# High-half products first, low-half products last within each weight piece of a two-layer decoder trunk

## The chip, the core and the metric

The kernel runs on one core of one Trainium2 chip. The metric is the device time of one execution in microseconds (us); the median of three runs is given, with the lowest and the highest beside it. Engines are called by the names of the profile: PE (TensorE, the matrix multiplier), PEld (its loads of the stationary operand), DVE (VectorE), ACT (ScalarE), POOL (GpSimd) and SP (SyncE, which issues most transfers here).

## What is computed

The reference is a decoder trunk with two layers over 256 tokens and a width of 2048, all in float32: a Mamba-2 state-space layer, one shared K/V projection, and a layer of dilated window attention. Almost all of the arithmetic is in seven projections; the rest works on their outputs.

```python
for layer in range(2):
    shift, scale, gate = adaln(c, ada_w[layer], ada_b[layer])       # silu(c) @ w + b, w: 2048 x 6144
    h = x * (1 + scale) + shift
    if layer == 0:                                                   # state-space layer
        z, xBC, dt = split(h @ in_w)                                 # 2048 x 10304
        xs, B, C = split(silu(causal_conv(xBC)))                     # depthwise, 4 taps
        y = ssd_scan(xs * dt, dt * A, B, C) + xs * D_skip            # 8 groups, one chunk of 256
        y = group_rms_norm(y * silu(z)) * norm_g @ out_w             # 4096 x 2048
    else:                                                            # attention layer
        q, z = split(h @ b_in_w)                                     # 2048 x 4096
        o = merge(dilated_attention(q[g], k[g], v[g]) for g in 3)    # by log-sum-exp weights
        y = (o * silu(z)) @ b_out_w                                  # 1024 x 2048
    x = layer_norm(alpha * x + (1 + gate) * y) * ln_g + ln_b
    if layer == 0:
        k, v = split(x @ kv_w)                                       # 2048 x 6144
```

## The kernel before

**Products in halves.** A float32 product is made of three products of the rounded format fp32r. Each operand is split into a high half (the value rounded) and a low half (what the rounding left): high x high, high x low and low x high are added up in one PSUM accumulator. The activations are split once, when they are made (tiles `hhi`/`hlo`, `xhi`/`xlo`, `yhi`/`ylo`, `oghi`/`oglo`, in the profile mostly `actT`). The weights are split as they arrive. `load_piece` (L90) issues a transfer of 512 KB from SP's queue into `raw` (six buffers), and `split` has ACT copy it into the high half `whi` (L100) and then DVE subtract that from `raw` into the low half `wlo` (L102). There are four buffers of each half. A buffer of `raw` is free again after the subtraction; a buffer of a half is free after the last matmul that reads it.

**Three forms of product.** A piece is the unit in which weights arrive and in which matmuls are issued.

- `cm_piece` (L151 to L153) gives columns by tokens: the weights are the stationary operand, the activations (256 tokens) move. A piece holds two k-tiles (`k`, rows of 128) of 512 output columns, in four blocks `n` of 128: 2 x 4 x 3 = 24 matmuls of 256 columns. The accumulator is two PSUM banks with two blocks each. Each block gets its three products one after the other.
- `cm_wide` (L182, L185) gives the same layout, for weights in pieces of four k-tiles and 256 columns. The high and low halves of the activations lie side by side, so one matmul of 512 columns (L182) makes two products, in the two halves of the block's bank; a matmul of 256 columns (L185) adds weight-low x activation-high. Per k-tile there are two of L182 and then two of L185, 16 matmuls a piece. At the end ACT and DVE add the halves of the bank (`put`).
- `tm_mults` (L213 to L215) gives tokens by columns: a block of 128 tokens of the activations is the stationary operand, and the weights (512 columns) move. A piece holds two k-tiles for two token blocks `b`, each with a bank of its own: 2 x 2 x 3 = 12 matmuls of 512 columns.

A product over all k-tiles is a loop over pieces with one accumulator pair (`cm_quad`, `cm_wide`, `tm_chunk`). The next product uses another pair; the pool `mm` has four banks. Near its end a product may begin the split of the next one's first piece (`begin_next`), and evictions are placed behind that split (`behind_next`) or put off into the next product (`later`, `owed`, `settle`).

**The opening stretch.** The first layer's activations `h` are not there at the start. Two columns of 1 MB of adaLN weights per k-tile are fetched, dotted with silu(c) on DVE (L295), and give shift and scale; ACT then writes `htmp` (L500) and the high half `hhi[kt]` (L502), and DVE the low half `hlo[kt]` (L504). Sixteen k-tiles come out one by one. Meanwhile a list written out by hand (`order`) says which pieces of which products use the k-tiles that are there. Each of its rows brings two more k-tiles into use. The names in it are the products: `z0`, `b4`, `x1` and so on, a dot marks the end of a part, whose sum is put away in SBUF (L633, L635), and the two `h` are the pieces of the first B/C and xs products. The last k-tiles are 14 and 15.

**The first layer's scan.** After the opening, `dt` goes through a softplus and a cumulative sum on DVE and small matmuls (L690 to L711); the cumulative rows are written to DRAM (`cumd`) and read back spread over the partitions (`cbc`). From these ACT makes the decay weights `seg` (L734, L736) of each group. `stage1` also transposes xs on PE (L745), and `stage2` makes the group's output (L767, L776). Both are placed between the products of the next groups.

**Order of issue.** The engines each run their instructions in a fixed order. It follows the program's order as far as a planner at build time, with costs of its own, finds the operands and buffers free; where the order matters it is pinned by `tc.issue_after`. So a transpose of a later step can stand between the matmuls of one piece.

Of the kernel before, what the change touches and what calls it, by code (L numbers as in the profile page):

```python
# [18 lines left out]
P = 128  # L19
# [30 lines left out]
def trunk(ctx, tc, xT, x, c, par, cst, bias, lnrow, ada, wdt, win, wxs, wout, wk, wv, wbin, wbout, out):  # L50
    nc = tc.nc
    V, S, T, PO = nc.vector, nc.scalar, nc.tensor, nc.gpsimd
# [35 lines left out]
    def load_piece(src):  # L88
        raw = wp.tile([P, 1024], F32, name="raw", bufs=6)
        nc.sync.dma_start(raw, src)  # L90
        return raw
# [5 lines left out]
    def split(raw, into=None, after=None, off=(0, 0)):  # L97

        hi, lo = into or halves_at(off)
        copied.append(S.activation(hi, raw, AF.Copy))  # L100
        with tc.issue_after(after) if after is not None else ExitStack():
            latest.append(V.tensor_tensor(lo, raw, hi.bitcast(F32), op=ALU.subtract))  # L102
        return hi.rearrange("p (k n) -> p k n", k=2), lo.rearrange("p (k n) -> p k n", k=2)
# [4 lines left out]
    def settle():  # L108

        while owed:  # L110
            with tc.issue_after(copied[-1].ins), tc.issue_after(latest[-1].ins):
                owed.pop(0)()

    def first_or(src, q, off=(0, 0)):

        return ready.pop() if ready else split(load_piece(src[q]), off=off)

    def begin_next():

        if upcoming:  # L120
            src, q, off = upcoming.pop(0)
            ready.append(split(load_piece(src[q]), off=off))

    def behind_next():

        stack = ExitStack()
        if ready:
            stack.enter_context(tc.issue_after(copied[-1].ins))
            stack.enter_context(tc.issue_after(latest[-1].ins))
        return stack  # L130

    def background(n, every=1):

        state[0] += n
        while state[0] >= every and jobs:
            state[0] -= every
            jobs.pop(0)()
# [3 lines left out]
    def cm_piece(src, q, ps, ahi, alo, k0=0, k1=KT, w=None, after=None, ks=(0, 1)):  # L141


        hi, lo = w or split(load_piece(src[q]), after=after, off=SHORT)
        for k in ks:
            kt = 2 * q + k
            for n in range(4):
                o = ps[n // 2][:, n % 2, :]
                c_ = slice(n * P, n * P + P)
                first = kt == k0 and n % 2 == 0  # L150
                T.matmul(o, hi[:, k, c_], ahi[:, kt, :], start=first, stop=False, skip_group_check=True)  # L151
                T.matmul(o, hi[:, k, c_], alo[:, kt, :], start=False, stop=False, skip_group_check=True)  # L152
                T.matmul(o, lo[:, k, c_], ahi[:, kt, :], start=False, stop=kt == k1 - 1, skip_group_check=True)  # L153

    def acc_pair(pool=None):
        return [(pool or mm).tile([P, 2, L], F32, name="acc") for _ in range(2)]
# [11 lines left out]
    def cm_wide(src, dst, rate=(0, 1), moving=None, later=False):  # L168

        both, high = moving or (lambda kt: xp[:, kt], lambda kt: xhi[:, kt, :])  # L170
        ps = acc_pair()
        for q in range(KT // 4):
            w = first_or(src, q, SHORT)
            if q == 1:
                settle()
            if q == KT // 4 - 1:
                begin_next()
            hi, lo = (t.rearrange("p k n -> p (k n)").rearrange("p (k n) -> p k n", k=4) for t in w)
            for k in range(4):
                kt = 4 * q + k  # L180
                for n in range(2):
                    T.matmul(ps[n], hi[:, k, n * P:n * P + P], both(kt), start=kt == 0, stop=False,  # L182
                             skip_group_check=True)
                for n in range(2):
                    T.matmul(ps[n][:, 0, :], lo[:, k, n * P:n * P + P], high(kt), start=False, stop=kt == KT - 1,  # L185
                             skip_group_check=True)
            background(*rate)
        def put():
            for n in range(2):
                S.activation(dst[:, n, :], ps[n][:, 1, :], AF.Copy)  # L190
                V.tensor_tensor(dst[:, n, :], ps[n][:, 0, :], dst[:, n, :], op=ALU.add)

        if later:
            owed.append(put)
        else:
            with behind_next():
                put()
# [7 lines left out]

    def tm_mults(q, w, ps, ahi, alo, k0, k1, blocks, cols=slice(0, 512)):
        hi, lo = (t[:, :, cols] for t in w)
        for k in range(2):
            kt = 2 * q + k
            for b in blocks:  # L210
                h_, l_ = ahi(kt)[:, b * P:b * P + P], alo(kt)[:, b * P:b * P + P]
                o, part = ps[b][:, cols], cols != slice(0, 512)
                T.matmul(o, h_, hi[:, k, :], start=kt == k0, stop=False, skip_group_check=part)  # L213
                T.matmul(o, h_, lo[:, k, :], start=False, stop=False, skip_group_check=part)  # L214
                end = T.matmul(o, l_, hi[:, k, :], start=False, stop=kt == k1 - 1, skip_group_check=part)  # L215
        return end

    def tm_pair():
# [115 lines left out]
    with ExitStack() as cA:  # L334
# [15 lines left out]
        with ExitStack() as cS:  # L350
# [78 lines left out]
            with ExitStack() as c0:  # L429
# [27 lines left out]
                first = [acc_pair(ex), acc_pair(ex)]  # L457
                cols = [(0, kind, kt) for kt in range(KT) for kind in ("scale", "shift")]
# [51 lines left out]
                part = {n: p[1:] for n, p in zip(names, begun.values())}  # L510
                two = "h"
                order = []
                for row in ("b4:0. b6:0. h z2:0. z1:0. b2:0 x1:0 h", "b2:1. x1:1. z1:1. z4:0 h h",
# [3 lines left out]
                    for w in row.split():  # L517
                        if w == two:
                            n = -2 if sum(o[0] == -2 for o in order) == sum(o[0] == -1 for o in order) else -1
# [117 lines left out]
                for i, (k, q, ends) in enumerate(order):  # L637
# [21 lines left out]
                    k0, k1 = (begin[k], 2 * q + 2 if ends else KT) if k in part else (0, KT)  # L659
# [178 lines left out]
            def y_to(ct):  # L838
                if ct < 4:
                    return [t[:, ct, :] for t in y_first]  # L840
                return yhi[ct // 16][:, ct % 16, :], ylo[ct // 4][:, ct % 4, :]
# [65 lines left out]
        for n in range(4):  # L907
            ps = tm_chunk(wout[n], lambda kt: y_to(kt)[0], lambda kt: y_to(kt)[1],
                          nk=2 * KT, rate=(1, 4) if n else (1, 2),
                          pre={0: y_ahead, 3: first_weights}.get(n), split_end=4 if n == 3 else 0)  # L910
# [67 lines left out]
    with ExitStack() as cL:  # L978
# [3 lines left out]
        def high(i, b):  # L982
            for k in range(2):
                kt = 2 * (i // 2) + k
                for w in first_v[i]:
                    T.matmul(vps[i % 2][b], hx(kt)[:, b * P:b * P + P], w[:, k, :], start=kt == 0 and w is first_v[i][0],  # L986
                             stop=False)
# [6 lines left out]
        end, _ = x_quad(0)  # L994
# [192 lines left out]
    for n in range(2):  # L1187
        ps = tm_chunk(wbout[n], *og, nk=H)
# [14 lines left out]
    ps = [tm_pair() for _ in range(2)]  # L1203
# [49 lines left out]
    end = last(1, 1, slice(256, 512), halves[1])  # L1253
# [124 lines left out]
```

## Time and profile before

| | before |
|---|---|
| median of three runs | 1235.47 us |
| lowest and highest | 1234.38 to 1236.19 us |
| profiled execution, span from first to last instruction | 1233.4 us |
| PE busy | 1219.2 us (99%), 7132 matmuls |
| PEld busy | 1048.7 us (85%), 7132 loads |
| DVE busy | 1027.8 us (83%) |
| ACT busy | 701.2 us (57%) |
| mean granted TensorE clock | 1.000 |
| HBM read | 331.45 MB, 271 GB/s over the span |

The page gives no time for the profiled execution but its span; the median of the runs is 2.1 us longer than that span. Matmuls are pipelined and their ends are modelled, so a busy share of 99% says that PE always had a matmul in hand, not that it ran at its peak; how fast it went is read from the steps between the starts of matmuls. In rows of the timeline the first number is the start, the second the time until the end of the group, and `x2` means that two neighbours are put together. In brackets stands the idle time ahead and what ended it.

### The profile page before, as it was taken

The page shows a single profiled execution, that of the slowest core. Times are in us where ns is not written, and L with a number is a line of the kernel's source. Part 1 is how long each engine was busy: PE and PEld are TensorE (multiplying, and loading weights), DVE is VectorE, ACT ScalarE, POOL GpSimd, SP SyncE. Part 2 cuts the span into 40 slices and gives each one's busy share as a digit, 9 for nine tenths or more (in the row PEclk, how much of TensorE's full clock was granted, in tenths as well). Part 3 has the DMA queues.
Part 4 walks back from the last instruction along what each step waited for, and adds up shares of the span by engine and source line. Part 5 has one row for each costly group of instructions (what it writes and reads, how often), then busy time and mean ns, then how long its engine had stood idle before and what let it go on. Part 6 is the DMA issues. An engine that isn't in the chain of part 4 may idle for free.

```text
span 1233.4 us, 18854 instructions
## 1 busy us (share of the span) xinstructions
PE 1219.2 (99%) x7132; PEld 1048.7 (85%) x7132; DVE 1027.8 (83%) x1464; ACT 701.2 (57%) x1048; POOL 3.9 (0%) x8
## 2 busy tenths in 40 slices
PE   8999999999999999999999999999999999999998
PEld 7889988898888888888888788888888888888886
DVE  6999986999988989899768678888978866758776
ACT  4554477878597789764335544434445644445551
POOL 0000000000000000000000000000000000000001
PEclk9999999999999999999999999999999999999999
DMA  9999977687656556698998569989998774464673
GB/s 377 423 420 422 421 255 248 224 299 252 215 199 209 168 171 205 217 338 345 362 316 293 196 202 372 347 344 371 382 384 306 232 256 144 122 199 128 206 257 69
DMA packets 81371, 335.92 MB, mean 272 GB/s; under 512 B 9200, under 2 KB 9984, under 8 KB 68480
## 3 DMA queue, kind: packets, MB, share of 16 engines
q1 hardware_dynamic: 80352, 333.33, 75.0%
q0 software_dynamic: 576, 1.05, 0.6%
q8 instruction: 56, 0.92, 0.3%
q10 hardware_dynamic: 352, 0.34, 0.1%
q14 instruction: 35, 0.29, 0.1%
HBM read 331.45 MB, written 3.23 MB: 271 GB/s over the span
## 4 chain that ended last, share of the span: by engine, by line
PE 81%; DMA 10%; DVE 6%; ACT 2%; issue 1%; DVEq 0%; ACTq 0%; SPq 0%
PE acc L182 24%; PE acc L185 12%; PE acc L214 11%; PE acc L215 11%; PE acc L213 11%; DMA raw<-in_win 5%; DMA araw<-in_ada 3%; DVE wlo L102 2%; DVE araw L295 2%; PE py L776 1%; ACT whi L100 1%; PE acc L151 1%; PE acc L153 1%; PE acc L152 1%; PE acc L986 1%
## 5 line engine op out<-in xcount | busy, mean ns | idle before, releaser
L100 ACT ACTIVATE whi<-raw 128x1024 fp32r<-128x1024 f32 x389 | 408.5, 1058 | 358.7 <-PE acc L215 128.9
L102 DVE TENSOR_TENSOR wlo<-raw,whi 128x1024 fp32r<-128x1024 f32 x389 | 469.2, 1220 | 147.8 <-ACT whi L100 139.1
L182 PE MATMUL acc<-actT,whi 128*128 128x512 f32 x1280 | 402.7, 394 | 0.0
L185 PEld LDWEIGHTS acc<-actT,wlo 128*128 128x128 f32 x1280 | 239.6, 188 | 53.5 <-DVE wlo L102 0.5
L214 PE MATMUL acc<-wlo,actT 128*128 128x512 f32 x656 | 257.4, 392 | 2.8 <-DVE wlo L102 2.8
L185 PE MATMUL acc<-actT,wlo 128*128 128x256 f32 x1280 | 253.8, 280 | 0.0
L213 PE MATMUL acc<-whi,actT 128*128 128x512 f32 x656 | 253.5, 394 | 0.0
L295 DVE SCALAR_TENSOR_TENSOR araw<-araw,cb__72 128x2048 f32<-128x2048 f32 x95 | 217.0, 2284 | 2.9 <-DMA araw<-in_ada 2.6
L182 PEld LDWEIGHTS acc<-actT,whi 128*128 128x128 f32 x1280 | 193.9, 188 | 0.4
L215 PE MATMUL acc<-whi,actT 128*128 128x512 f32 x432 | 168.8, 391 | 0.0
L214 PEld LDWEIGHTS acc<-wlo,actT 128*128 128x128 f32 x656 | 123.2, 188 | 30.3 <-DVE wlo L102 5.1
L213 PEld LDWEIGHTS acc<-whi,actT 128*128 128x128 f32 x656 | 122.6, 188 | 24.2
L151 PE MATMUL acc<-actT,whi 128*128 128x256 f32 x372 | 103.1, 281 | 1.5 <-ACT actT L502 0.9
L153 PE MATMUL acc<-actT,wlo 128*128 128x256 f32 x372 | 101.9, 282 | 1.3 <-DVE wlo L102 1.1
L152 PE MATMUL acc<-actT,whi 128*128 128x256 f32 x372 | 103.1, 280 | 0.0
L215 PEld LDWEIGHTS acc<-whi,actT 128*128 128x128 f32 x432 | 81.1, 188 | 16.5
L215 PE MATMUL acc<-whi,ylo 128*128 128x512 f32 x224 | 87.6, 391 | 0.0
L151 PEld LDWEIGHTS acc<-actT,whi 128*128 128x128 f32 x372 | 69.6, 188 | 2.8 <-ACT actT L502 1.3
L153 PEld LDWEIGHTS acc<-actT,wlo 128*128 128x128 f32 x372 | 68.9, 188 | 2.5 <-DVE wlo L102 2.3
L152 PEld LDWEIGHTS acc<-actT,whi 128*128 128x128 f32 x372 | 70.6, 190 | 0.2
L215 PEld LDWEIGHTS acc<-whi,ylo 128*128 128x128 f32 x224 | 42.1, 188 | 8.5
L734 ACT ACTIVATE seg<-cbc,cumT 128x128 f32<-128x128 f32 x128 | 41.1, 389 | 3.5 <-PE py L776 2.1
(311 smaller groups left out, 1151.8 us busy)
## 6 DMA issues: line engine op xcount, KB each, us to landing
araw<-in_ada SPq DMA_DIRECT2D x96, 1024.0 KB, 7.2
raw<-in_win SPq DMA_DIRECT2D x109, 512.0 KB, 6.5
raw<-in_wout SPq DMA_DIRECT2D x64, 512.0 KB, 5.6
raw<-in_wbin SPq DMA_DIRECT2D x64, 512.0 KB, 3.8
raw<-in_wxs SPq DMA_DIRECT2D x48, 512.0 KB, 4.4
raw<-in_wv SPq DMA_DIRECT2D x48, 512.0 KB, 7.2
raw<-in_wk SPq DMA_DIRECT2D x48, 512.0 KB, 7.8
cbc<-cumd SPq DMA_DIRECT2D x16, 512.0 KB, 5.4
```

The source lines that it names most:

```text
L100: copied.append(S.activation(hi, raw, AF.Copy))
L102: latest.append(V.tensor_tensor(lo, raw, hi.bitcast(F32), op=ALU.subtract))
L151: T.matmul(o, hi[:, k, c_], ahi[:, kt, :], start=first, stop=False, skip_group_check=True)
L152: T.matmul(o, hi[:, k, c_], alo[:, kt, :], start=False, stop=False, skip_group_check=True)
L153: T.matmul(o, lo[:, k, c_], ahi[:, kt, :], start=False, stop=kt == k1 - 1, skip_group_check=True)
L182: T.matmul(ps[n], hi[:, k, n * P:n * P + P], both(kt), start=kt == 0, stop=False, skip_group_check=True)
L185: T.matmul(ps[n][:, 0, :], lo[:, k, n * P:n * P + P], high(kt), start=False, stop=kt == KT - 1, skip_group_check=True)
L213: T.matmul(o, h_, hi[:, k, :], start=kt == k0, stop=False, skip_group_check=part)
L214: T.matmul(o, h_, lo[:, k, :], start=False, stop=False, skip_group_check=part)
L215: end = T.matmul(o, l_, hi[:, k, :], start=False, stop=kt == k1 - 1, skip_group_check=part)
L295: return V.scalar_tensor_tensor(raw, raw, 1.0, cb_, op0=ALU.mult, op1=ALU.mult, accum_out=mod[layer][:, ct, j:j + 1])
L734: S.activation(seg[:, hh, b, :], cbc[:, hh, b, :], AF.Relu, bias=cumT[:, b, h0 + hh:h0 + hh + 1], scale=-1.0)
```

## The change

Within a piece the loops are turned inside out. The outermost loop now goes over the kinds of product, and those with the weights' low half are last:

- `cm_piece`: all weight-high x activation-high of the piece (8 matmuls), then all weight-high x activation-low (8), then all weight-low x activation-high (8).
- `cm_wide`: the eight matmuls of 512 columns with the high half for the four k-tiles, then the eight of 256 columns with the low half.
- `tm_mults`: all activation-high x weight-high (4 for two token blocks), then all activation-low x weight-high (4), then all activation-high x weight-low (4). Before, the weight-low product stood second of the three.

The number of matmuls, their operands, their shapes and the accumulators are the same. The start flag stays on the first matmul into a bank.

```diff
 cm_piece
-        for k in ks:
-            kt = 2 * q + k
-            for n in range(4):
-                o = ps[n // 2][:, n % 2, :]
-                c_ = slice(n * P, n * P + P)
-                first = kt == k0 and n % 2 == 0
-                T.matmul(o, hi[:, k, c_], ahi[:, kt, :], start=first, stop=False, skip_group_check=True)
-                T.matmul(o, hi[:, k, c_], alo[:, kt, :], start=False, stop=False, skip_group_check=True)
-                T.matmul(o, lo[:, k, c_], ahi[:, kt, :], start=False, stop=kt == k1 - 1, skip_group_check=True)
+        for w_, a_ in ((hi, ahi), (hi, alo), (lo, ahi)):
+            for k in ks:
+                kt = 2 * q + k
+                for n in range(4):
+                    begins = w_ is hi and a_ is ahi and kt == k0 and n % 2 == 0
+                    T.matmul(ps[n // 2][:, n % 2, :], w_[:, k, n * P:n * P + P], a_[:, kt, :], start=begins,
+                             stop=w_ is lo and kt == k1 - 1, skip_group_check=True)
 cm_wide
                 for n in range(2):
                     T.matmul(ps[n], hi[:, k, n * P:n * P + P], both(kt), start=kt == 0, stop=False,
                              skip_group_check=True)
+            for k in range(4):
+                kt = 4 * q + k
                 for n in range(2):
                     T.matmul(ps[n][:, 0, :], lo[:, k, n * P:n * P + P], high(kt), start=False, stop=kt == KT - 1,
                              skip_group_check=True)
 tm_mults
-        for k in range(2):
-            kt = 2 * q + k
-            for b in blocks:
-                h_, l_ = ahi(kt)[:, b * P:b * P + P], alo(kt)[:, b * P:b * P + P]
-                o, part = ps[b][:, cols], cols != slice(0, 512)
-                T.matmul(o, h_, hi[:, k, :], start=kt == k0, stop=False, skip_group_check=part)
-                T.matmul(o, h_, lo[:, k, :], start=False, stop=False, skip_group_check=part)
-                end = T.matmul(o, l_, hi[:, k, :], start=False, stop=kt == k1 - 1, skip_group_check=part)
+        part = cols != slice(0, 512)
+        for a_, w_ in ((ahi, hi), (alo, hi), (ahi, lo)):
+            for k in range(2):
+                kt = 2 * q + k
+                for b in blocks:
+                    end = T.matmul(ps[b][:, cols], a_(kt)[:, b * P:b * P + P], w_[:, k, :],
+                                   start=a_ is ahi and w_ is hi and kt == k0, stop=w_ is lo and kt == k1 - 1,
+                                   skip_group_check=part)
```

## The prediction

> **What bounds the kernel now.** I read the page first (busy time, chain, groups), then the table by stage, the waits of TensorE and its weight loads, and last the timeline at the few places where those waits fall.
>
> ```profile
> span 1233.4 us, 18854 instructions
> PE 1219.2 (99%) x7132; PEld 1048.7 (85%) x7132; DVE 1027.8 (83%) x1464; ACT 701.2 (57%) x1048; POOL 3.9 (0%) x8
> PE 81%; DMA 10%; DVE 6%; ACT 2%; issue 1%; DVEq 0%; ACTq 0%; SPq 0%
> ...
> L182 PE MATMUL acc<-actT,whi 128*128 128x512 f32 x1280 | 402.7, 394 | 0.0
> ```
>
> TensorE (PE) is busy 99% of the span and carries 81% of the chain that ended last. The order of its matmuls, which is all that changes, is therefore worth what it does to two things: the steps from one matmul's start to the next, and the few waits. PE has as many weight loads (PEld) as matmuls, so no load is shared between neighbours now, and none can be lost. The last row gives the number of wide pieces: a piece of `cm_wide` holds 8 matmuls of L182, so there are 1280 / 8 = 160.
>
> By stage (PE, PEld, DVE, ACT, POOL busy; clock, DMA share, GB/s):
>
> ```profile
> 20.40:164.00 143.60, 140.01 (x959) 128.61 (x960) 133.97 (x146) 79.07 (x103) 0.00 (x0) 1.00 1.00 410
> 164.00:223.00 59.00, 56.98 (x350) 50.28 (x349) 43.97 (x78) 45.70 (x69) 0.00 (x0) 1.00 0.76 260
> 223.00:580.00 357.00, 356.62 (x2347) 302.32 (x2348) 332.72 (x556) 265.74 (x454) 0.00 (x0) 1.00 0.68 232
> 700.00:945.00 245.00, 244.67 (x1272) 208.38 (x1272) 205.78 (x226) 112.60 (x144) 0.00 (x0) 1.00 0.90 340
> ```
>
> The opening stretch is another regime than the rest: DMA is full (share 1.00, 410 GB/s) and VectorE (DVE) is busy 134.0 of 143.6 us. From 223 us on PE alone sets the time. The waits of the weight loads and of PE (total us, times, longest):
>
> ```profile
> PEld acc L214 <- DVE wlo L102: 5.1, 6, 1.3
> PEld acc L153 <- DVE wlo L102: 2.3, 5, 0.8
> ...
> PEld acc L185 <- DVE wlo L102: 0.5, 2, 0.4
> ```
>
> These are the waits for a low half. Today the second (L214) or third (L153) matmul of a piece needs it. In all 5.1 + 2.3 + 0.5 = 7.9 us: the most that moving the low half last can free.
>
> **The change part by part: removed and added.** No instruction, load, DMA or byte is added or taken away; inside a piece the same products run in another order. Of a plain piece (24 matmuls of 256 columns, or 12 of 512) the low half is needed after two thirds instead of after one or two matmuls. The high half comes free after two thirds, so ScalarE (ACT) may overwrite that buffer earlier; the low half comes free at the end as before, or one step later. Nothing new waits on SP or POOL.
>
> **Step 1, the pace.** Steps from start to start, by rows a known number of steps apart. First the wide form:
>
> ```profile
> 799.62 0.62 PE L182 MATMUL acc<-actT,whi 128*128 128x512 f32 x2
> 800.08 0.39 PE L185 MATMUL acc<-actT,wlo 128*128 128x256 f32 x2
> ...
> 810.02 0.62 PE L182 MATMUL acc<-actT,whi 128*128 128x512 f32 x2
> ```
>
> Fifteen k-steps of two 512-column and two 256-column matmuls take 10.40 us, 0.6933 each. Streams of one width alone are the token-major form (30 steps) and `cm_piece` at two places (60 steps each):
>
> ```profile
> 640.06 0.39 PE L214 MATMUL acc<-wlo,actT 128*128 128x512 f32 x1
> ...
> 646.86 0.39 PE L214 MATMUL acc<-wlo,actT 128*128 128x512 f32 x1
> ```
>
> ```profile
> 199.84 0.28 PE L152 MATMUL acc<-actT,whi 128*128 128x256 f32 x1
> ...
> 206.90 0.28 PE L152 MATMUL acc<-actT,whi 128*128 128x256 f32 x1
> ```
>
> ```profile
> 246.78 0.28 PE L153 MATMUL acc<-actT,wlo 128*128 128x256 f32 x1
> ...
> 253.58 0.28 PE L153 MATMUL acc<-actT,wlo 128*128 128x256 f32 x1
> ```
>
> That is 0.2267 us a matmul of 512, and 0.1177 or 0.1133 of 256: one code ran at two paces. A wide piece changes from four times (512, 512, 256, 256) to eight of 512 and then eight of 256, so it should come near the pure streams: 8 x 0.2267 + 8 x 0.1177 = 2.755 us against 4 x 0.6933 = 2.773. That is 0.018 us a piece, 160 x 0.018 = 2.9 us less. At the faster pace of 256 it is 8 x 0.2267 + 8 x 0.1133 = 2.720, 0.053 a piece, 8.5 us less. The other end: today's k-step split as 0.2267 x 2 and the rest, 0.2399, over two narrow ones would give each of those 0.1200, and the new order would then gain nothing. I take 2.8, by the slower pace, since today's narrow steps, 0.1200 by that split, are nearest to it; an end below nothing is rival D.
>
> The Trainium skill, page "TensorE: Matmul & The Clock Gate", section "Back-to-back issue gap", gives a step by the matmul's own width alone, about 216 ns for 512 columns and 109 for 256, so the mix would not matter and the gain here would be nothing. The trace is slower than that throughout (0.227 and 0.113 to 0.118), and at 0.6933 its mixed stream is above its pure ones.
>
> `cm_piece` and the token-major form keep their widths, so I put their pace at no change. In the latter every matmul will change its PSUM bank, not every third; the 30 steps above hold ten changes, and the wide form, which changes at each matmul, takes 800.08 - 799.62 = 0.46 us for a wide pair, two of those steps: nothing. The 256-column products of `cm_piece` number 3 x 372 = 1116 (the rows of L151 to L153 in the table of groups), and may fall into either pace: at most 1116 x 0.0044 = 4.9 us either way, if all went from one to the other.
>
> ```profile
> L151 PE MATMUL acc<-actT,whi 128*128 128x256 f32 x372 | 103.1, 281 | 1.5 <-ACT actT L502 0.9 <-ACT s L635 0.6
> ```
>
> **Step 2, the waits after 223 us.** Two low-half waits stand in the PE-bound part:
>
> ```profile
> 578.64 0.39 PE L213 MATMUL acc<-whi,actT 128*128 128x512 f32 x1
> 579.40 0.50 PE L214 MATMUL acc<-wlo,actT 128*128 128x512 f32 x1 [0.38 <-DVE wlo L102]
> 579.74 0.39 PE L215 MATMUL acc<-whi,ylo 128*128 128x512 f32 x1
> ...
> 926.71 0.61 PE L213 MATMUL acc<-whi,actT 128*128 128x512 f32 x2
> 927.65 0.50 PE L214 MATMUL acc<-wlo,actT 128*128 128x512 f32 x1 [0.33 <-DVE wlo L102]
> 927.99 0.40 PE L215 MATMUL acc<-whi,actT 128*128 128x512 f32 x1
> ```
>
> The first loses 0.76 - 0.23 = 0.53 us, and 0.34 - 0.23 = 0.11 on the step behind it; the second 0.94 - 2 x 0.23 = 0.48, and 0.11. In the new order eight high-half matmuls, 8 x 0.2267 = 1.8 us, run before the low half is asked for: both go, 1.2 us in all. What is late next is the following piece's low half, which DVE subtracts directly behind (1.2 us a piece against 2.7 us of matmuls). The 0.5 us of L185 adds at most that; I leave it.
>
> **Step 3, the opening stretch.** Here most of the waits stand, and here I count nothing. The new order needs the low half later, but the second k of a piece earlier: after 4 matmuls instead of 12 in `cm_piece`, after 2 instead of 6 in the other form. These activations come out one by one behind DVE's adaLN dots, and the last odd one decides:
>
> ```profile
> 157.71 0.60 ACT L500 ACTIVATE htmp<-xt,mod 128x256 f32<-128x256 f32 x1 [3.10 <-DVE mod L300]
> 158.34 0.42 ACT L502 ACTIVATE actT<-htmp 128x256 fp32r<-128x256 f32 x1
> ```
>
> ```profile
> 157.95 0.28 PE L151 MATMUL acc<-actT,whi 128*128 128x256 f32 x1
> 158.06 0.28 PE L152 MATMUL acc<-actT,whi 128*128 128x256 f32 x1
> 158.87 0.38 PE L153 MATMUL acc<-actT,wlo 128*128 128x256 f32 x1 [0.54 <-DVE wlo L102]
> ```
>
> Now this piece (kt 14 and 15) starts at 157.95, waits for its low half until 158.87, and has 22 matmuls left: 158.87 + 0.11 + 22 x 0.1177 = 161.57. In the new order it starts sooner, as the earlier low-half waits are gone, runs four matmuls and waits for kt 15, which ACT delivers at 158.34 + 0.42 = 158.76; 20 are left: 158.81 + 20 x 0.1177 = 161.16. Whatever PE gained before is handed to that wait. The gain is 0.4 us, not the 5 or so that the stretch's waits add up to. The delivery is fixed by DVE and the full DMA, not by PE.
>
> Even this 0.4, and the low-half wait at 187.7, do not reach the end, since a second gate follows:
>
> ```profile
> 187.71 0.50 PE L214 MATMUL acc<-wlo,actT 128*128 128x512 f32 x1 [0.45 <-DVE wlo L102]
> ```
>
> ```profile
> 183.44 1.37 DVE L633 TENSOR_TENSOR s<-acc,s 128x512 f32<-128x512 f32 x2
> ```
>
> ```profile
> 196.68 3.56 DMA cumd<-araw
> 200.26 4.83 DMA cbc<-cumd
> ```
>
> ```profile
> 205.12 1.57 ACT L734 ACTIVATE seg<-cbc,cumT 128x128 f32<-128x128 f32 x5 [1.38 <-DMA cbc<-cumd]
> ```
>
> ```profile
> PE aux L745 <- DVE cb L724: 1.6, 1, 1.6
> ```
>
> ```profile
> 222.91 0.63 PE aux L745 x4
> ```
>
> PE stands 1.6 us at L745 (222.9 us) for work that hangs on the decay rows' trip through DRAM and on ACT, which itself sat idle for them. That trip starts behind DVE's eviction at L633. In the token-major form the first bank now ends one matmul before the piece's end instead of three, 2 x 0.2267 = 0.45 us later; less the 0.4 gained, the eviction starts where it did. In other products that 0.45 is hidden, since the next one fills the other pair of banks. So up to 223 us I take 0, between -1.6 us (the wait gone) and +0.45 (no gain, and the eviction late).
>
> **The sum.** -2.8 - 1.2 + 0 = -4.0 us on the span of 1233.4: 1229.4. The page has no other time of that execution; the median of 1235.47 lies 2.1 above the span, for what lies around it. Predicted: 1235.47 - 4.0 = 1231.5.
>
> **Rivals.**
> A. Only the waits count; width changes cost nothing (the 0.1200 case). 1235.47 - 1.2 = 1234.3, inside what a measurement can tell from no change (0.2%, 2.5 us). For it: 0.018 us a piece is a difference of averages. Against: the mixed k-step is above both pure paces. The page's rule above would lead here too.
> B. The narrow run of `cm_wide` falls into the fast pace: -8.5 - 1.2 = 1225.8. For it: 246 to 254 us shows it held for 60 steps. Against: 199 to 207 does not.
> C. The opening is not gated: earlier free buffers let transfers and DVE run ahead, and most of the 7.9 us of low-half waits is saved: 1235.47 - 2.8 - 7.9 = 1224.8. Against: DMA share 1.00 and DVE at 93% there.
> D. The slower side: in `cm_wide` a 512-column matmul costs more when it directly follows one of another k. Today a narrow pair stands between; afterwards each piece has three such joints. At 0.020 us each, with nothing gained in step 1, 160 x 3 x 0.020 = 9.6, less 1.2: 1243.9. It decides (over +2.5 us) from 3.7 / 480 = 0.008 us a joint. Against: in the token-major form the moving operand changes from step to step too, at 0.2267 throughout.
>
> **How the numbers follow.** Forecast 0.52, A 0.22, B 0.08, C 0.05, D 0.13. The forecast's own range is 1229.5 to 1233.5 (step 1 at 1 to 4 us, `cm_piece` within 1 of its pace); a tenth of its chance lies above 1233.0. Faster: 0.47 + 0.08 + 0.05 = 0.60; same: 0.05 + 0.22 = 0.27; slower 0.13. The range for 8 in 10 takes in A and half of B and of D's small prices: 1226.5 to 1236.5.
>
> **What would show it.** The wide k-steps in two runs, a piece at about 2.755 us; no L214, L153 or L185 wait after 223 us; in the opening, waits of L151 or L213 on ACT's actT at odd kt in place of the low-half waits, the last one ending near 158.8; PE still waiting at L745 near 223. I am wrong if the piece of `cm_wide` is at 2.773 or above, if kt 15 arrives much before 158.8, or if the order of transposes and evictions between the pieces comes out differently and opens new waits.

## The result, and the profile after

| | before | changed |
|---|---|---|
| median of the runs beside each other | 1234.38 us (1233.39 to 1236.19) | 1243.15 us (1241.52 to 1246.48) |
| ratio, 95% interval | | 1.0071 [1.0058, 1.0085] |
| span of the profiled execution | 1233.4 us | 1244.7 us (its time: 1246.48 us) |
| mean granted TensorE clock | 1.000 | 0.995 |

The change makes the kernel 8.8 us slower; 1231.5 was forecast, and 1236.5 was the upper end of the range. The profiled execution of the changed kernel is the longest of its five, 3.3 us above their median, so the places found in it are somewhat dearer than on average; the experiments below are compared by medians.

The page of the changed kernel, the lines that answer to those shown of before:

```profile
span 1244.7 us, 18860 instructions
PE 1224.7 (98%) x7132; PEld 1051.7 (84%) x7132; DVE 1029.6 (83%) x1464; ACT 703.1 (56%) x1050; POOL 3.9 (0%) x8
PE 85%; DMA 7%; DVE 4%; ACT 2%; issue 1%; DVEq 0%; ACTq 0%; SPq 0%
```

The work is the same: 7132 matmuls and as many loads. PE is busy 5.5 us longer with it and idle 5.8 us more. By stage (columns as before: PE, PEld, DVE, ACT, POOL busy; clock, DMA share, GB/s):

```profile
20.40:164.00 143.60, 138.69 (x941) 127.50 (x942) 132.33 (x143) 76.69 (x103) 0.00 (x0) 0.99 1.00 408
164.00:223.00 59.00, 56.31 (x356) 50.33 (x355) 40.52 (x70) 42.75 (x66) 0.00 (x0) 1.00 0.74 248
223.00:580.00 357.00, 352.31 (x2305) 297.07 (x2306) 328.33 (x554) 269.30 (x457) 0.00 (x0) 0.99 0.65 223
700.00:945.00 245.00, 244.45 (x1274) 207.72 (x1273) 204.84 (x240) 111.20 (x147) 0.00 (x0) 1.00 0.86 323
```

The first and the third stage hold fewer matmuls than before (941 against 959, 2305 against 2347), both at a clock of 0.99; the second holds a few more (356 against 350). The last one, where only products run, has not lost anything (1274 against 1272). Where the lateness arises shows from single instructions that both kernels have, by their start (us):

| | before | changed | later by |
|---|---|---|---|
| transposition of dt (L624) | 171.52 | 173.67 | 2.2 |
| transposition of the cumulative rows (L701) | 194.45 | 199.47 | 5.0 |
| L767 of group 0 | 229.11 | 233.01 | 3.9 |
| L767 of group 5 | 456.88 | 462.36 | 5.5 |
| L767 of group 7 | 512.11 | 524.99 | 12.9 |
| end of the span | 1233.4 | 1244.7 | 11.3 |

So about 3.9 us are lost up to 229 us, 1.6 on the way to 457, 7.4 between 457 and 512 us, and 1.6 come back behind it. These figures are rough, since such a step need not stand between the same products in both kernels. PE's waits in these places, in the timeline of the changed kernel (start, time, in brackets the idle time ahead and what ended it):

```profile
157.04 0.62 PE L150 MATMUL acc<-actT,whi 128*128 128x256 f32 x4
159.49 0.75 PE L150 MATMUL acc<-actT,whi 128*128 128x256 f32 x4 [1.83 <-ACT actT L502]
...
224.10 0.62 PE L745 MATMUL aux<-cc,xs 128*128 128x128 f32 x4 [3.79 <-DVE cb L724]
...
502.72 0.63 PE L745 MATMUL aux<-cc,xs 128*128 128x128 f32 x4 [1.57 <-DVE cb L724]
504.52 0.41 PE L829 MATMUL aux<-cc,s 128*128 128x128 f32 x2 [1.17 <-DVE xo L755]
505.73 1.98 PE L776 MATMUL py<-xd,seg 128*64 128x64 f32 x32 [0.80 <-DVE seg L737]
```

And the granted clock in those places (after the busy times stands PEclk):

```profile
156.66:160.08 3.42, 1.59 (x14) 1.39 (x13) 3.20 (x5) 1.66 (x3) 0.00 (x0) 1.00 0.62 201
160.08:163.49 3.41, 3.41 (x19) 3.41 (x18) 2.36 (x2) 1.47 (x3) 0.00 (x0) 0.50 0.64 173
221.53:224.94 3.41, 0.84 (x6) 0.83 (x7) 3.41 (x6) 3.41 (x6) 0.00 (x0) 1.00 0.80 267
224.94:228.35 3.41, 3.41 (x10) 2.63 (x9) 3.41 (x9) 2.51 (x3) 0.00 (x0) 0.50 0.10 41
501.42:504.83 3.41, 0.94 (x6) 0.62 (x6) 3.33 (x8) 3.38 (x6) 0.00 (x0) 1.00 0.01 2
504.83:511.66 6.83, 6.03 (x43) 4.80 (x43) 6.41 (x13) 5.15 (x14) 0.00 (x0) 0.50 0.28 79
```

Behind the waits in each of these three places the clock falls to half, twice for 3.41 us and once for 6.83. At half clock a stretch does half its work, so these 13.65 us cost up to 6.8. The kernel before had no such stretch (clock 1.000), though it too waited once here, 1.57 us ahead of 222.9 us.

### The profile page after: what moved, and what is told of

The parts are those of the page before. It is cut to its first block, busy times and chain, and to the rows that moved or that the text cites. A ratio compares the mean times of both kernels' runs of the same rounds, so it can differ in the third digit from the quotient of the medians.

```text
span 1244.7 us, 18860 instructions
## 1 busy us (share of the span) xinstructions
PE 1224.7 (98%) x7132; PEld 1051.7 (84%) x7132; DVE 1029.6 (83%) x1464; ACT 703.1 (56%) x1050; POOL 3.9 (0%) x8
## 4 chain that ended last, share of the span: by engine, by line
PE 85%; DMA 7%; DVE 4%; ACT 2%; issue 1%; DVEq 0%; ACTq 0%; SPq 0%
PE acc L213 38%; PE acc L180 24%; PE acc L185 12%; DMA raw<-in_win 5%; PE acc L150 3%; DVE araw L295 2%; PE py L776 1%; DVE wlo L102 1%; DMA araw<-in_ada 1%; ACT whi L100 1%; PE acc L986 1%; DMA cbc<-cumd 1%; DMA adab<-in_par 1%; PE po L1124 1%; PE aux L1101 1%
## 5 line engine op out<-in xcount | busy, mean ns | idle before, releaser
L180 PE MATMUL acc<-actT,whi 128*128 128x512 f32 x1280 | 328.3, 396 | 0.0
L213 PE MATMUL acc<-whi,actT 128*128 128x512 f32 x1088 | 280.1, 394 | 0.0
L180 PEld LDWEIGHTS acc<-actT,whi 128*128 128x128 f32 x1280 | 228.2, 188 | 42.1
L185 PEld LDWEIGHTS acc<-actT,wlo 128*128 128x128 f32 x1280 | 170.5, 188 | 14.3
L213 PE MATMUL acc<-wlo,actT 128*128 128x512 f32 x656 | 180.5, 395 | 0.9 <-DVE wlo L102 0.9
L185 PE MATMUL acc<-actT,wlo 128*128 128x256 f32 x1280 | 173.9, 277 | 0.0
L150 PE MATMUL acc<-actT,whi 128*128 128x256 f32 x744 | 96.7, 282 | 4.8 <-ACT actT L502 3.7
L150 PEld LDWEIGHTS acc<-actT,whi 128*128 128x128 f32 x744 | 91.8, 190 | 6.6 <-ACT actT L502 4.5
L213 PE MATMUL acc<-whi,ylo 128*128 128x512 f32 x224 | 61.6, 391 | 0.0
L150 PE MATMUL acc<-actT,wlo 128*128 128x256 f32 x372 | 52.4, 284 | 0.1
L734 ACT ACTIVATE seg<-cbc,cumT 128x128 f32<-128x128 f32 x128 | 41.0, 390 | 14.7 <-PE py L776 9.2
L150 PEld LDWEIGHTS acc<-actT,wlo 128*128 128x128 f32 x372 | 47.7, 192 | 0.7 <-DVE wlo L102 0.7
L368 DVE SCALAR_TENSOR_TENSOR cacc<-xs,prm,cacc 128x255 f32<-128x255 f32 (+2 forms) x72 | 30.6, 480 | 0.8 <-ACT cacc L365 0.7
L776 PEld LDWEIGHTS py<-xd,seg 128*64 128x64 f32 x512 | 16.9, 143 | 8.9 <-issue 4.5
```

Of the source, the lines that this page charges most:

```text
L150: T.matmul(ps[n // 2][:, n % 2, :], w_[:, k, n * P:n * P + P], a_[:, kt, :], start=begins, stop=w_ is lo and kt == k1 - 1, skip_group_chec ...
L213: end = T.matmul(ps[b][:, cols], a_(kt)[:, b * P:b * P + P], w_[:, k, :], start=a_ is ahi and w_ is hi and kt == k0, stop=w_ is lo and kt ...
L368: V.scalar_tensor_tensor(acc[:, o:], ps[:, :L - o], w[:, j:j + 1], acc[:, o:], op0=ALU.mult, op1=ALU.add)
L734: S.activation(seg[:, hh, b, :], cbc[:, hh, b, :], AF.Relu, bias=cumT[:, b, h0 + hh:h0 + hh + 1], scale=-1.0)
L776: T.matmul(py[t_, e_], segs[hh // 4][:, hh % 4, b, t_], xd[:, b, e_], start=True, stop=True)
```

## The experiments

Each kernel below was run beside the kernel before; medians, and the ratio with its 95% interval. The kernels with the new order in some places only hold both orders in the three functions and choose by a table that is switched at three points of the program:

```diff
+    new = dict.fromkeys(('cm', 'wide', 'tm'), OPENING)
...
+            new.update(dict.fromkeys(new, SCAN))
...
+        new.update(dict.fromkeys(new, LATER))
```

The first line holds up to the end of the opening list, the second stands at the first pool of the scan, the third behind the scan. In e5, e6, e8, e11, e12 and e13 single forms are set besides.

| run | what has the new order, or what else | median | before | ratio |
|---|---|---|---|---|
| e1 | opening list alone | 1239.65 | 1234.45 | 1.0041 [1.0028, 1.0055] |
| e2 | scan alone | 1243.36 | 1234.45 | 1.0080 [1.0066, 1.0094] |
| e3 | all behind the scan | 1234.06 | 1234.45 | 0.9996 [0.9987, 1.0005] |
| e4 | everything, with filler in three waits | 1242.93 | 1234.45 | 1.0073 [1.0060, 1.0085] |
| e5 | wide pieces of the scan alone | 1241.93 | 1234.50 | 1.0058 [1.0044, 1.0072] |
| e6 | everything but those | 1238.86 | 1234.50 | 1.0032 [1.0021, 1.0044] |
| e7 | everything, group 6 traced early | 1236.16 | 1234.50 | 1.0013 [1.0004, 1.0022] |
| e8 | cm pieces of the opening list | 1237.64 | 1234.50 | 1.0025 [1.0014, 1.0035] |
| e9 | from the scan on, group 6 early | 1235.89 | 1234.63 | 1.0009 [1.0000, 1.0018] |
| e10 | nothing, group 6 early | 1235.40 | 1234.63 | 1.0005 [0.9996, 1.0014] |
| e11 | as e8, but kt 14 and 15 old | 1234.19 | 1234.63 | 0.9996 [0.9987, 1.0005] |
| e12 | tm pieces of the opening list | 1237.88 | 1234.63 | 1.0027 [1.0018, 1.0037] |
| e13 | e3 and e11 together | 1233.98 | 1234.54 | 0.9996 [0.9987, 1.0005] |
| e14 | nothing, group 6 held back | 1239.81 | 1234.32 | 1.0044 [1.0030, 1.0057] |

**Which stretch (e1, e2, e3).** One of the three switches on in each. The theories told apart are waits (at kt 15 and in the scan), the pace of the pieces, and the scan's steps standing in other places.

> The new order in the opening stretch alone (the hand-written list of pieces, up to 164 us); the old one in the scan and after it. Theory W (new waits bunched on PE, each followed by a stretch at half clock, plus a changed order of the other engines in the scan): the wait for kt 15 and the half clock at 160 us return and PE is 2.2 us late at 164; the gate near 223 us takes in 1.6 of that, so +0.5 to +1.5 us on the whole, clock 0.998 to 0.999. Theory P (the new order runs at a slower pace of matmuls everywhere): 58 of some 330 pieces, +1.5 us, clock 1.000. Theory S (the planner's changed order in the scan alone is to blame): 0.

> The new order in the products of the scan stage alone (164 to 540 us). Theory W: the second and third half-clock stretch (near 225 and 505 us) and the waits around them return: +5 to +7 us, clock 0.997. Theory P: about a third of the pieces, +3 us, clock 1.000. Theory S: +7 to +9 us, all of the loss, with most of it in waits of PE and not in the clock.

> The new order from the first layer's output projection on (540 us to the end), 112 of the 160 wide pieces among it. Theory W: nothing but the two low-half waits that go (579 and 927 us), -1.2 us, clock 1.000. Theory P: some 60% of the pieces, +5 us. My prediction's step 1 would give 112 x 0.018 = 2.0 us more gain, -3.2 us.

Pace would have shown most in e3, which covers more than half of the span and came out at the kernel before. The losses are in e1 (+5.2) and e2 (+8.9), in stretches where other engines' steps stand between the products. e1 lost far more than the 0.5 to 1.5 us expected from waits there. e2's loss lies in the range of theory S, though a part of it is clock: the half clock near 501 us came back (6.83 us long, so up to 3.4 us), the one near 225 us did not. The parts add up to 13.7, and the whole lost 8.8: they share something.

**The clock (e4).** The changed kernel, with matmuls that add zero (8, 14 and 12 of them) in front of the three waits:

```diff
+    def fill(n, out, mov, start):
+
+        for i in range(n):
+            T.matmul(out[i % 2], nought, mov, start=start and i < 2, stop=False, skip_group_check=True)
```

> The changed kernel, with matmuls that add zeros set ahead of the three places where PE waited before its clock halved: 8 of 512 columns before kt 15 is first used, 14 before the second z product, 12 in the last z product. They compute nothing and replace idle time by work: 1.8, 3.2 and 2.7 us, about as long as the waits. Theory W, with the clock falling because PE was idle: the half-clock stretch at 160 us goes, those near 225 and 505 go or shrink, clock 0.998 to 1.000, and the time falls by 2 to 5 us against the changed kernel although 7.7 us of matmuls are added (1238 to 1241 us, +0.3 to +0.5% on before). If the clock falls for another reason than idle time (or at fixed times): clock stays at 0.995 to 0.997 and the added work shows, 1243 to 1250 us.

The window of e4 over the whole disputed stretch:

```profile
150.00:600.00 450.00, 445.71 (x2880) 379.32 (x2879) 403.63 (x659) 323.24 (x535) 0.00 (x0) 1.00 0.68 237
```

The clock stays at 1.00 here, and over each of e4's five executions its mean is 0.998 to 1.000, against 0.995 to 0.997 in the changed kernel: it was the idle time that halved it. The time bears out neither theory. With the clock restored 1238 to 1241 was expected, and the total did not move (1242.93 against 1243.15). 34 filler matmuls at 0.227 us are 7.7 us; it may be that what the waits do not hide of that, with the waits that remain (1.65 us for cb at 223.7 us), eats up what the clock gave back, but no run separates the two. The half clock follows the waits, so it adds to the loss and is not its origin.

**The place of group 6 (e5, e6, e7, e14).** What differs in 457 to 512 us besides the order inside the pieces is where the scan's own steps stand between them. In the kernel before group 6's last outputs (L767) and group 7's first scores (L720) start 8.5 us apart, in the changed kernel 2.0. PE before:

```profile
483.68 1.02 PE L767 MATMUL aux<-xo,cb 128*128 128x512 f32 x2
484.63 2.08 PE L776 MATMUL py<-xd,seg 128*64 128x64 f32 x64
492.22 0.59 PE L720 MATMUL aux<-bcm 128*128 128x256 f32 x2
```

and after:

```profile
497.30 1.02 PE L767 MATMUL aux<-xo,cb 128*128 128x512 f32 x2
498.25 1.15 PE L776 MATMUL py<-xd,seg 128*64 128x64 f32 x32
499.33 0.70 PE L720 MATMUL aux<-bcm 128*128 128x256 f32 x2
```

One step earlier, group 6's first scores (L720) start at 463.2 us before, in the middle of group 7's xs product, and at 487.6 in the changed kernel, behind all of it. DVE then has two groups' work at once, and PE reaches its transpositions with nothing to do between them. The engines' orders are fixed when the program is built, by the planner described above, which weighs operands and buffers by costs of its own; another order of matmuls inside the pieces gave it another answer. Of the three forms, the wide one in the scan moves group 6: with the new order there alone (e5) its first scores start at 481.0 us, behind all of the xs product, and with the new order everywhere else (e6) at 469.8, in the middle of it.

> The new order only in the wide pieces of the scan; every other product in the old order. The program's order of PE puts group 6's first score product (L720) behind the whole xs product of group 7, as in the changed kernel, instead of in its middle, so that group 6's second half and group 7's first half come together. Theory of placement: the 457 to 512 us stretch loses its 5 to 7 us in waits on cb and xo and a half-clock stretch near 500 us, 1239.5 to 1242. Theory of pace and release (the pieces themselves cost): the wide pieces' pace is 2.77 us as before, so nothing, 1233.5 to 1235.

> The changed kernel with the old order in the wide pieces of the scan alone; all other pieces in the new order. Group 6's first score product stands in the middle of the xs product of group 7 again. Theory of placement: the loss at 457 to 512 us goes, the loss of the opening stays (about +5), less 1 for the waits at 579 and 927 us: 1237 to 1239. Theory that the tm and cm pieces' own order starves the scan: still 1241.5 to 1244.

Both fell where the theory of placement had them, 1241.9 and 1238.9. The wide pieces' pace was the old one (2.77 us in e5), so it was not they that cost. The traces say the same of the stretch itself: from L767 of group 5 to L767 of group 7 it takes 55.2 us before and 54.3 in e6, but 62.6 in the changed kernel, 62.5 in e2 and 62.9 in e5.

e7 keeps all of the change and traces the first half of group 6 (`stage1`), with `stage3` of group 5 ahead of it, between the two wide halves of that product:

```diff
+                    if w and mid is not None:
+                        mid()
...
+                def between():
                     stage3(g - 1, rs)
+                    early.extend(stage1(g))
+
+                product("xs", g + 1, between if g == G - 2 else None)
```

> The changed kernel, all three forms new, but the trace of the program puts the first half of group 6's scan (L720 to L753) between the two wide halves of group 7's xs product, so that PE meets it some 10 us earlier than in the changed kernel. Theory of placement: no wait on cb or xo above 0.8 us and no half clock at 499 to 506 us, 1236 to 1239.5. Theory that the new matmul order itself costs: 1241.5 to 1244.

7.0 of the 8.8 us came back, with every matmul of the pieces in the new order: between 221 and 698 us its trace has no wait of PE above 0.3 us and no half clock after 223 us, and the stretch between the two L767 takes 54.7 us.

Up to 472 us every engine of e7 runs the changed kernel's instructions in the changed kernel's order, and yet L767 of group 0 starts at 228.82 us in its profiled execution, not at 233.01. The kt 15 wait was as long (1.84 us), but no half clock followed it, and group 0's wait for cb was 2.29 us instead of 3.79. So what the same order loses in the opening differs by some 4 us between these two executions, and the two traces alone could not price the move; the medians, 7.0 us apart, and the stretch between the two L767 do.

e14 is the reverse: the old order everywhere, and only this place held back.

```diff
-                st1 = stage1(g)
+                with tc.issue_after(end_wide[0].ins) if g == G - 2 else ExitStack():
+                    st1 = stage1(g)
```

> The kernel before, all matmuls of the pieces in the old order, with one pin: the matmuls and transposes of the first half of group 6's scan are held behind the last matmul of group 7's xs product, where the changed kernel has them. Theory of placement (the place alone makes the loss at 457 to 512 us): waits on cb and seg of 2 us or more in all near 495 us, a stretch of half clock behind them, 1239 to 1242. Theory that the new order of the matmuls is needed for the loss: 1234 to 1235.5.

It lost 5.5 us. Its waits there, 0.7 to 1.1 us each and 2.6 in all, are for xo, seg and a low half where cb and seg were expected; they fall together, and the clock drops behind them. The timeline of PE and two windows of e14:

```profile
498.42 0.41 PE L831 MATMUL aux<-cc,s 128*128 128x128 f32 x2 [1.07 <-DVE xo L756]
499.64 1.45 PE L777 MATMUL py<-xd,seg 128*64 128x64 f32 x32 [0.81 <-DVE seg L738]
```

```profile
498.79:502.20 3.41, 1.82 (x36) 1.35 (x35) 3.40 (x8) 3.41 (x12) 0.00 (x0) 1.00 0.03 5
502.20:505.62 3.42, 3.42 (x8) 2.77 (x9) 3.01 (x7) 1.69 (x3) 0.00 (x0) 0.50 0.57 153
```

Ahead of 467 us its other engines keep the order of the kernel before, and the stretch between the two L767 takes 61.4 us. So the place of these steps alone makes most of the loss at 457 to 512 us, and moving it takes that loss away. e10 shows that the early place is no gain by itself, and e9 what is left of the scan's loss with it:

> The kernel before with group 6's first half traced early and nothing else. Theory that the early place only repairs what the new order displaced: 1234 to 1235.5. Theory that the early place is a gain by itself (e7's recovery would then not be the displaced steps): 1230 to 1233.

> The old order in the opening, the new one from the scan on, and the first half of group 6's scan traced between the two wide halves of group 7's xs product as in e7. If the loss is the opening's wait on kt 15 plus the place of group 6, both are gone and what is left is the gain of the two low-half waits: 1231.5 to 1234. If the scan in the new order costs something beside group 6's place: 1235 to 1237.

e9 missed the first theory: 1.3 us stay. In its trace the waits stand at group 0, where PE waits 2.18 us for cb ahead of 220.7 us (1.57 before) and 0.99 for xo ahead of 229.1 (none before); no run isolates them.

**The opening (e8, e11, e12).** Here only the forms of the opening list change.

> The new order only in the cm pieces of the opening list; the scan's steps stand where the kernel before has them. PE still needs kt 15 early near 157 us. Theory of the gate (the wait of 1.8 us at kt 15 and the half clock behind it cost, whatever the planner does): dt arrives 1.4 to 2.2 us later and it stays, 1235.8 to 1237. Theory of placement (what is lost is lost behind 164 us by the other engines' order): dt is up to 1.5 us late but the scan makes it up, 1234 to 1235.3.

> As e8, the new order in the cm pieces of the opening list, but the pieces with kt 14 and 15 in the old order. The steps of the scan stand where the kernel before has them. Theory of the gate: PE asks for kt 15 as late as before, no half clock near 160 us, dt on time, 1234 to 1235.2. Theory that the release of the cm pieces' halves costs: 1236.5 to 1238 as e8.

> The new order only in the tm pieces of the opening list. PE asks for kt 15 when it did before; the order of the scan's steps is that of e1. e1 lost 5.2 and e8 3.1 us, so the theory of two separate losses has this one at 1236 to 1237.5; the theory that all of the opening's loss is the gate has it at 1234 to 1235.2.

e11's time is the one that the theory of the gate at kt 15 gives it; e8's 1237.64 lies above the ranges of both theories. The traces do not bear the gate out. In e8's execution PE waited 0.92 us at kt 15, the clock held there, and dt was transposed at 171.49 us, as before (171.52). It lost 3.0 us only at group 0's cb, and the reason is on DVE, where the steps of the scan did not stay where the kernel before has them. e8 (L758 and L759 are the two writes of cb, L402 convolutions, L103 splits, L455 evictions):

```profile
217.12 1.23 DVE L103 TENSOR_TENSOR wlo<-raw,whi 128x1024 fp32r<-128x1024 f32 x1 [4.14 <-ACT whi L101]
218.26 0.69 DVE L455 TENSOR_TENSOR s<-acc,s 128x512 f32<-128x512 f32 x1
219.01 1.23 DVE L103 TENSOR_TENSOR wlo<-raw,whi 128x1024 fp32r<-128x1024 f32 x1
220.15 0.68 DVE L455 TENSOR_TENSOR s<-acc,s 128x512 f32<-128x512 f32 x1
220.75 2.84 DVE L402 SCALAR_TENSOR_TENSOR cacc<-s,prm,cacc 128x255 f32<-128x255 f32 x7
223.51 0.41 DVE L758 TENSOR_TENSOR cb<-aux,cc 128x256 f32<-128x256 f32 x1
223.84 0.47 DVE L402 SCALAR_TENSOR_TENSOR cacc<-s,prm,cacc 128x254 f32<-128x254 f32 x1
224.24 0.28 DVE L759 COPY cb<-aux 128x128 f32<-128x128 f32 x1
```

and e11, with the same line numbers:

```profile
216.72 1.23 DVE L103 TENSOR_TENSOR wlo<-raw,whi 128x1024 fp32r<-128x1024 f32 x1 [0.67 <-PE acc L165]
217.86 1.28 DVE L455 TENSOR_TENSOR s<-acc,s 128x512 f32<-128x512 f32 x2
219.06 0.41 DVE L758 TENSOR_TENSOR cb<-aux,cc 128x256 f32<-128x256 f32 x1
219.40 2.84 DVE L402 SCALAR_TENSOR_TENSOR cacc<-s,prm,cacc 128x255 f32<-128x255 f32 x7
222.16 0.28 DVE L759 COPY cb<-aux 128x128 f32<-128x128 f32 x1
```

In e8 a split stands between the two evictions and the first write of cb behind the convolutions; cb is complete 2.1 us later, PE waits 2.6 us for it, and the clock halves from 225.80 to 229.21. In e11 every instruction of DVE, ACT, SP and POOL stands in the order of the kernel before, though the cm pieces but those of kt 14 and 15 have the new order, and nothing is lost. e11 thus clears the new order itself, in these pieces, of the loss; it does not separate kt 15 from the displaced steps, since leaving kt 14 and 15 alone restored both. e12 has no new demand for kt 15, no half clock, and lost 3.3 us, a little above the range of two separate losses: group 0's steps are moved here too (2.55 us of wait for cb ahead of 219.4, 1.51 for xo ahead of 228.0). e8 and e12 wait at the same instruction for the same tile, which may be why e1, with both, lost 5.2 and not 6.4.

**Both harmless parts (e13).**

> The two parts that did no harm by themselves, together: the new order in the cm pieces of the opening list but for kt 14 and 15 (e11), and in all products behind the scan (e3); the tm and wide pieces up to the end of the scan in the old order. Theory that only the two low-half waits near 579 and 927 us are to be had: 1233.2 to 1234.3. Theory that the small steps of e3 and e11 below the kernel before (0.4 and 0.4 us) are nothing but spread: 1234.3 to 1235.

0.6 us below the kernel before, inside the interval: it does not tell the two theories apart, and no version here is shown to beat the kernel before. Both low-half waits at 579 and 927 us are gone, but a transposition behind the scan (L864) now waits 0.5 us for DVE, so of 1.2 us about half is left.

## Why the prediction was wrong

**Step 1, the pace: the term was mis-sized, 0 instead of -2.8.** Four wide pieces of the changed kernel:

```profile
819.95 2.02 PE L180 MATMUL acc<-actT,whi 128*128 128x512 f32 x8
821.81 1.07 PE L185 MATMUL acc<-actT,wlo 128*128 128x256 f32 x8
...
831.04 0.62 PE L180 MATMUL acc<-actT,whi 128*128 128x512 f32 x2
```

They take 831.04 - 819.95 = 11.09 us, 2.773 a piece, what four old k-steps of 0.6933 took. The eight narrow ones run at the fast pace, (822.72 - 821.81) / 8 = 0.114 us, but the eight wide ones at (821.81 - 819.95) / 8 = 0.2325 and not at the 0.2267 borrowed from the token-major form. The outcome of the 0.1200 case, rival A, was the true one for this step. With the pace also go rivals B and D: D's joints between wide matmuls may cost 0.006 us each, and the narrow ones give it back. "Back-to-back issue gap", on the Trainium skill's page "TensorE: Matmul & The Clock Gate", which let the mix not matter, had the right outcome, though these steps stay above its 216 and 109 ns.

**Step 2, the two low-half waits: right in place and size.** Both are gone in the changed kernel, and from L767 of group 7 to the end it needs 719.7 us against 721.3. In e3 and e13 half of it is given back at one transposition.

**Step 3, the opening: the step that failed.** Its mechanism was there: four matmuls, then the wait for kt 15 (the rows at 157.04 and 159.49). It was put at nothing, between -1.6 and +0.45 us; the opening alone measured +5.2 (e1). Two things were missing. First, a wait was priced at its own length. Earlier the idle time was strewn over several low-half waits of half a microsecond; gathered into 1.83 us it was followed here by 3.41 us at half clock, another 1.7 (in e7's execution it was not). Second, the chain up to L745 was moved rigidly, as if DVE's and ACT's orders stayed. They did not: the cumulative rows are transposed 5.0 us later, though dt is only 2.2 late, the DRAM trip's first read is awaited longer, and the ACT and DVE steps behind it pile up. From the timelines of ACT and DVE of the changed kernel:

```profile
211.92 0.40 ACT L734 ACTIVATE seg<-cbc,cumT 128x128 f32<-128x128 f32 x1 [5.36 <-DMA cbc<-cumd]
```

```profile
221.00 1.23 DVE L102 TENSOR_TENSOR wlo<-raw,whi 128x1024 fp32r<-128x1024 f32 x1 [6.47 <-ACT whi L100]
222.14 1.28 DVE L421 TENSOR_TENSOR s<-acc,s 128x512 f32<-128x512 f32 x2
223.34 0.41 DVE L723 TENSOR_TENSOR cb<-aux,cc 128x256 f32<-128x256 f32 x1
```

L734 began at 205.12 before, after 1.38 us of waiting, and the first write of cb (L723) at 219.39; here they are 6.8 and 4.0 us later.

**What had no step at all.** The largest loss, 457 to 512 us, lies in the stretch for which the prediction read from the table by stage that PE alone sets the time. That reading failed: with group 6's steps moved, PE waits there for DVE's cb, xo and seg. Among the ways to be wrong stood that "the order of transposes and evictions between the pieces comes out differently and opens new waits", without a price. e7 puts it at 7.0 us, e14, without the new order, at 5.5. The slower rival, D, had the sign, and its 1243.9 is close to the measured 1243.15 by luck: its cause, a wide piece that grows dearer at its joints, is not what the runs show.

**Still open.** Which of the planner's costs turned, and whether the kt 15 wait would cost anything with all other engines' orders held as before; no run had the one without the other.

## What to carry to other kernels

Where a planner at build time orders the engines, a change inside one loop can move steps that the diff does not touch: compare the orders of all engines before and after, and price the moved steps, before the loop itself. A busy share of 99% does not protect a stretch whose steps hang on other engines; count how far apart two groups' dependent steps stand. To learn what the edit itself is worth, run it where the other engines' order comes out unchanged (e11, for the cm pieces of the opening), and run the displaced order without the edit (e14).

## What had not been expected of the hardware

- Behind one wait of 1.83 us (PE busy 1.59 of the 3.42 us ahead) the clock fell to half, and in e14 behind two waits of 1.07 and 0.81 us in one stretch (busy 1.82 of 3.41). The Trainium skill, page "TensorE: Matmul & The Clock Gate", section "Why this matters for your kernels", warns of idle gaps above some 3 us; by these rows less can be enough.
- The length of a wait alone does not decide it: 1.83 us ahead of 221.19 us in e2, 1.84 ahead of 158.82 in e7 and 2.55 ahead of 219.39 in e12 passed at full clock. In the changed kernel the three falls lie 64.86 and 279.89 us apart, which is 19 and 82 times 3.413. The Trainium skill, page "TensorE: Matmul & The Clock Gate", section "What's actually happening", has a free-running window of 3413 ns, and these distances and the lengths of 3.41 and 6.83 us agree with it. Counted back in such steps from each run's next fall, e7's wait is shared by two of them, the first two rows below, while e2's lies within one, the third:

```profile
154.90:158.31 3.41, 2.08 (x16) 1.70 (x15) 3.38 (x5) 0.59 (x1) 0.00 (x0) 1.00 0.81 315
158.31:161.72 3.41, 2.90 (x25) 2.90 (x26) 2.88 (x4) 2.86 (x6) 0.00 (x0) 1.00 0.60 181
217.95:221.36 3.41, 1.58 (x9) 1.01 (x8) 3.27 (x6) 3.41 (x6) 0.00 (x0) 1.00 0.84 268
```

  The third has PE less busy than e14's 1.82 of 3.41, and still no half clock followed. So where a wait falls seems to matter, but PE's busy time as the profile has it does not settle it; the rule stays open.
- Steps of 512 columns ran at 0.2325 us in the wide form and 0.2267 in the token-major one, without a wait in either.
